# Every engine's attention and layer-norm steps in written order, and a rotation that multiplies in place

## The chip, the cores and the metric

The kernel runs on one core of one Trainium2 chip. The metric is the device time of one launch in microseconds (us). The kernel before was run three times: 1959.72, 1959.80 and 1962.09 us, median 1959.8.

## The reference

One step of a hybrid encoder layer for T = 320 token rows (256 of a prompt, 64 of a running sample), D = 2048, all in float32:

```python
xn = rmsnorm(x); h = xn @ w_in                      # columns [u | v | q | k | v_attn]
u, v = gelu(h[u]), gelu(h[v])                        # 2048 columns each
q, k = rope(h[q]), rope(h[k])                        # 32 query heads, 4 key heads, 64 wide; 16 rotated
a = u * (masked_ws @ layernorm(v) + bs)              # the gMLP branch, chunks of 128 rows
o = sink_softmax(q k^T / 8) v_attn                   # window of 128 keys and the own chunk of 64
x = x + (sigmoid(xn@w_gate_a) * (a @ w_branch_a) + sigmoid(xn@w_gate_b) * (o @ w_branch_b)) @ w_out
x = x + (silu(n@w_ffn_gate) * (n@w_ffn_up)) @ w_ffn_down,  n = rmsnorm(x);  y = rmsnorm(x)
```

The new keys, the new values and the normalised v rows of the sample are outputs too.

## The kernel before

Activations lie transposed, features on the partitions and the 320 rows along the free axis. Each weight product is three matmuls: a float32 operand is split into a rounded high part and the low rest (`xh`, `xl` for the activations, `hi`, `lo` for the weights), and hi·xh, hi·xl and lo·xh are added up in PSUM (L167 to L169).

**Blocks.** `gemm` (L151) makes 512 output columns with four PSUM banks. It goes through the 2048 inputs in eight blocks of 256, and a block is 24 matmuls. The weights of all products stand in one list `plan`, and block j uses entry j. At the start of block j ScalarE rounds the high part of entry j+2 (`high`, L134); after the first 12 matmuls VectorE subtracts to get the low part (`low`, L143) and SyncE fetches entry j+6 (`fetch`, L123). So a weight is to be ready two blocks ahead of its use.

**Slots.** After every 12 matmuls `pump` (L96) runs the functions that `later(n, fn)` has put n slots ahead. This calendar spreads the attention over the running products, two slots to a block. The products come in this order: kv, q0, q1, v0, q2, v1, q3, v2, v3 (list `QV`, L37), then the four of gate b (gb0 to gb3). Blocks are numbered from 0 through all of them, eight to a product, so v0 is blocks 24 to 31, q2 32 to 39, v1 40 to 47, q3 48 to 55, v2 56 to 63, v3 64 to 71, gb0 72 to 79.

**Attention.** A step (g, n) is key head g and chunk n of 64 rows, 20 steps in all, 5 slots apart within a g. `attend` (L475) places its parts at slots 0 to 16: scores on TensorE into two banks (slot 0), row maxima on VectorE (1, L492, then `nm` L494 and `es` L496), exponentials on ScalarE (2, L505, L508; these free the two banks), division on VectorE (3, L514 to L519) and ScalarE (4, L521), a transpose into `u` on VectorE (5, L527), four writes of `u` to DRAM by SyncE's queue (6, L536) and the read back as `pf` (8, L545), its high part on ScalarE (11, L557, L565) and low part on VectorE (12, L560, L568), the value matmuls on TensorE into one bank (14, L575), a copy `ol` on ScalarE (15, L579) and two additions into `f1` on VectorE (16, L587; these free the bank). When a q product ends, ScalarE copies it to `qr` (L600) and issues four small transfers that swap the two rotated halves into `swp` (L346, L347); at slots 5 and 7 VectorE turns two column tiles each (`rope_turn`, L349), and ScalarE and VectorE make the split queries `qs` (L467, L471). When a v product ends, VectorE scales it out of its four banks (L622), ScalarE applies Gelu (L625), and TensorE turns the four tiles (L630) into banks that VectorE and ScalarE copy out one slot later (L635, L636).

**Banks and rings.** There are eight PSUM banks: four for the running product and four for all else, the banks of the product before among them until they are copied out. The SBUF ring `st` has two buffers; `pf`, `ol` and `rope_t1` take them in turn.

**Layer norm.** During gb1 to gb3 `split_o` (L666) splits the attention's output, `v_aggr` (L670) and `v_norm` (L684) normalise v, `v_load` (L677) fetches gains and offsets, and `load_ws` (L691) and `turn_ws` (L699) fetch and turn the spatial weights.

**Order.** Inside `tc.manual_schedule()` every engine issues its instructions in the order in which the program writes them. In the kernel before this holds to the end of the kv product (L446). After it a scheduler orders each engine's instructions by its own forecast of when they can run: it takes the earliest written one that is ready by that forecast, so it moves instructions ahead of others that would wait. The order so fixed is what the chip runs.

Of the kernel before, what the change touches and what calls it, by code (L numbers as in the profile page):

```python
# [10 lines left out]
F32 = mybir.dt.float32  # L11
F32R = mybir.dt.float32r
AF = mybir.ActivationFunctionType
ALU = mybir.AluOpType
# [4 lines left out]
P = 128  # L19
D = 2048  # L20
DC = D // P
T = 320
# [47 lines left out]
def tile_hybrid_step(ctx: ExitStack, tc: tile.TileContext, a: dict, outs: list):  # L70
    nc = tc.nc
# [7 lines left out]
    tmp = ctx.enter_context(tc.tile_pool(name="tmp", bufs=2))  # L79
# [10 lines left out]
    def later(slots, fn):  # L90
        calendar.setdefault(now[0] + max(1, slots), []).append(fn)

    startup = tc.manual_schedule()
    startup.__enter__()

    def pump():  # L96
        now[0] += 1
        for fn in calendar.pop(now[0], []):
            fn()

    def flush():
        while calendar:
            pump()
# [47 lines left out]
    def gemm(w, c0, xh, xl, name, k0=0, nk=DC, nt=4):  # L151
        ps = [bank(f"mm_{name}_{t}") for t in range(nt)]
        for kb in range(0, nk, 2):
            j = at_block[0]
            at_block[0] += 1
            assert plan[j][1:] == (c0, k0 + kb, nt)
            ahead = j + PARTS - 1
            todo = ahead not in parts
            if todo:
                high(ahead)  # L160
            hi, lo = parts.pop(j)
            for t in range(nt):
                cols = slice(t * P, (t + 1) * P)
                for c in range(2):
                    k = kb + c
                    o = ps[t][:, :T]
                    nc.tensor.matmul(o, hi[:, c, cols], xh[:, k, :], start=(k == 0), stop=False)  # L167
                    nc.tensor.matmul(o, hi[:, c, cols], xl[:, k, :], start=False, stop=False)  # L168
                    nc.tensor.matmul(o, lo[:, c, cols], xh[:, k, :], start=False, stop=(k == nk - 1))  # L169
                if t == 1:  # L170
                    if todo:
                        low(ahead)
                    fetch(ahead + RAWS)
                if t % 2 == 1:
                    pump()
        return [p[:, :T] for p in ps]
# [163 lines left out]
    swp = ap.tile([P, 4, T], F32, name="swp")  # L340
    nc.gpsimd.memset(swp, 0.0)
    qr = ap.tile([P, 4, T], F32, name="qr")
# [4 lines left out]
            nc.scalar.dma_start(swp[b + 8 : b + 16, 0:nt, :], qr[b : b + 8, 0:nt, :])  # L347

    def rope_turn(t0):  # L349
        t1 = tmp.tile([P, 2, T], F32, tag="st", name="rope_t1")  # L350
        cb = cos_t.unsqueeze(1).broadcast_to([P, 2, T])
        sb = sin_t.unsqueeze(1).broadcast_to([P, 2, T])
        q2 = qr[:, t0 : t0 + 2, :]
        nc.vector.tensor_tensor(q2, q2, cb, op=ALU.mult)
        nc.vector.tensor_tensor(t1, swp[:, t0 : t0 + 2, :], sb, op=ALU.mult)
        nc.vector.tensor_tensor(q2, q2, t1, op=ALU.add)

    ka = ap.tile([P, 4, NPOS], F32R, name="ka")
    kl = ap.tile([P, 4, NPOS], F32R, name="kl")
# [83 lines left out]
            split_v64(5, v, 0)  # L443

    ps = gemm(w_in, 3 * D, xh, xl, "kv")
    startup.__exit__(None, None, None)  # L446
    for t in range(4):
        nc.scalar.activation(qr[:, t, :], ps[t], AF.Copy)
    later(1, lambda: rope_swap(2))
# [1 line left out]
    for i, n in xs:  # L451
        later(6 + i, lambda i=i, n=n: new_v(i, i * P, n))
        later(8 + 2 * i, lambda i=i: v_blocks(i))
    later(6, lambda: rope_turn(0))
    later(9, k_out)
    later(9, rope_scale)
# [141 lines left out]
    def q_done(g, ps):  # L598
        for t in range(4):
            nc.scalar.activation(qr[:, t, :], ps[t], AF.Copy)  # L600
        qs = ap.tile([P, 20, 2, 64], F32R, tag="qs", name=f"qs_{g}")
        hi, lo = q_parts(g, qs)
        later(1, lambda: rope_swap(4))
        later(5, lambda: rope_turn(0))
        later(7, lambda: rope_turn(2))
        at = QK0[g]
        later(at - 5, lambda: hi(0))
        later(at - 4, lambda: lo(0))
        later(at - 3, lambda: hi(1))
        later(at - 2, lambda: lo(1))  # L610
        for n in range(5):
            for dt, step in attend(g, n, qs, {}):
                later(at + 5 * n + dt, step)
# [107 lines left out]
    def sigmoid(dst, ps, b0, g):  # L721
        for t in range(4):
            m = 4 * g + t
            z = dst(m)
            nc.vector.tensor_tensor(z, ps[t], rx, op=ALU.mult)
            nc.scalar.activation(z, z, AF.Sigmoid, bias=vec[:, b0 + m : b0 + m + 1])
# [8 lines left out]
    for g in range(1, 4):  # L735
        sigmoid(gate_b, gemm(w_gate, D + g * W, xh, xl, f"gb{g}"), 80, g)
    flush()
    yh, yl = late["yh"], late["yl"]
    for g in range(4):
        ps = gemm(w_bb, g * W, yh, yl, f"bb{g}")  # L740
# [234 lines left out]
```

## Time and profile before

| | |
|---|---|
| median of three runs | 1959.8 us |
| the profiled execution | 1959.65 us, of which its span is 1957.5 us |
| TensorE busy | 1930.3 us (99%) |
| VectorE busy | 1041.6 us (53%) |
| ScalarE busy | 813.5 us (42%) |
| mean granted TensorE clock | 0.995 |
| read from HBM | 292.15 MB |

Times in the rows are microseconds from the start of the span, "mean ns" is one instruction's duration, "x" a count. PE is TensorE, PEld its weight loads, DVE VectorE, ACT ScalarE, SP SyncE; SPq and ACTq are those engines' queues of instructions and transfers. A row of the waits reads: who waited, for whom, us in total, times, the longest. L numbers are lines of the kernel.

### The profile page before, as it was taken

How to read it: one execution, taken by the hardware profiler on the slowest of the kernel's cores; microseconds unless marked ns; L12 is line 12 of the kernel's file. 1: busy time of each engine (PE TensorE's matmuls, PEld its weight loads, DVE VectorE, ACT ScalarE, POOL GpSimd, SP SyncE). 2: the span in 40 equal slices, each digit the busy share in tenths (PEclk: the TensorE clock that was granted, in tenths of full speed). 3: DMA queues.
4: the chain of work that ended last, by engine and by line, in shares of the span. 5: the costliest groups of instructions: out<-in, count | busy, mean ns of one | idle time of the engine just before them, and what ended most of it. 6: DMA issues, size and time to landing. Idle time of an engine off the chain costs nothing.

```text
span 1957.5 us, 31779 instructions
## 1 busy us (share of the span) xinstructions
PE 1930.3 (99%) x13179; PEld 1922.1 (98%) x13179; DVE 1041.6 (53%) x1527; ACT 813.5 (42%) x1220; POOL 4.7 (0%) x12
## 2 busy tenths in 40 slices
PE   8999999999999999999999999999999999999996
PEld 8999999999999999999999999999999999999996
DVE  5778887944354544455454434443444444444454
ACT  5566776533233343334343333333333333333343
POOL 0000000000000000000000000000000000000000
PEclk9999999999999999999999999999999999999998
DMA  8556666754444444445455555444555444555433
GB/s 261 162 161 184 175 179 177 225 159 146 149 143 136 140 151 151 151 150 203 147 149 151 151 151 151 151 150 147 148 150 150 150 151 151 151 151 149 149 129 103
DMA packets 169456, 307.41 MB, mean 157 GB/s; under 512 B 11312, under 2 KB 28672, under 8 KB 169120
## 3 DMA queue, kind: packets, MB, share of 16 engines
q1 hardware_dynamic: 164256, 293.64, 49.1%
q10 hardware_dynamic: 5056, 11.74, 1.9%
q8 instruction: 103, 1.69, 0.4%
q14 instruction: 41, 0.34, 0.0%
HBM read 292.15 MB, written 12.45 MB: 156 GB/s over the span
## 4 chain that ended last, share of the span: by engine, by line
PE 83%; DVE 1%; ACT 1%; DMA 1%; issue 0%; DVEq 0%; SPq 0%; ACTq 0%
PE mm_fd L169 5%; PE mm_fd L167 5%; PE mm_fu L167 5%; PE mm_fg L167 5%; PE mm_fg L168 5%; PE mm_fu L169 5%; PE mm_fg L169 5%; PE mm_fu L168 5%; PE mm_fd L168 5%; PE mm_u L167 2%; PE mm_ba L169 2%; PE mm_bb L167 2%; PE mm_ba L168 2%; PE mm_bb L168 2%; PE mm_ga L169 2%; PE mm_wo L169 2%
## 5 line engine op out<-in xcount | busy, mean ns | idle before, releaser
L143 DVE TENSOR_TENSOR lo<-raw,hi 128x1024 fp32r<-128x1024 f32 (+1 forms) x534 | 646.4, 1211 | 667.5 <-ACT hi L134 666.1
L134 ACT ACTIVATE hi<-raw 128x1024 fp32r<-128x1024 f32 (+1 forms) x533 | 559.3, 1050 | 1022.0 <-PE mm_fu L168 188.8
L167 PE MATMUL mm_fd<-xh,hi 128*128 128x320 f32 x704 | 218.2, 310 | 0.0
L167 PE MATMUL mm_fg<-yh,hi 128*128 128x320 f32 x704 | 217.8, 309 | 0.0
L168 PE MATMUL mm_fu<-yl,hi 128*128 128x320 f32 x704 | 217.6, 309 | 0.0
L169 PE MATMUL mm_fg<-yh,lo 128*128 128x320 f32 x704 | 217.6, 309 | 0.0
L168 PE MATMUL mm_fg<-yl,hi 128*128 128x320 f32 x704 | 217.6, 309 | 0.0
L167 PE MATMUL mm_fu<-yh,hi 128*128 128x320 f32 x704 | 217.6, 309 | 0.0
L169 PE MATMUL mm_fu<-yh,lo 128*128 128x320 f32 x704 | 217.6, 309 | 0.0
L169 PE MATMUL mm_fd<-xh,lo 128*128 128x320 f32 x704 | 217.1, 308 | 0.0
L168 PE MATMUL mm_fd<-xl,hi 128*128 128x320 f32 x704 | 217.1, 308 | 0.0
L168 PEld LDWEIGHTS mm_fg<-yl,hi 128*128 128x128 f32 x704 | 132.2, 188 | 0.1
L167 PEld LDWEIGHTS mm_fg<-yh,hi 128*128 128x128 f32 x704 | 132.2, 188 | 0.1
L167 PEld LDWEIGHTS mm_fu<-yh,hi 128*128 128x128 f32 x704 | 132.2, 188 | 0.0
L169 PEld LDWEIGHTS mm_fu<-yh,lo 128*128 128x128 f32 x704 | 132.2, 188 | 0.0
L169 PEld LDWEIGHTS mm_fg<-yh,lo 128*128 128x128 f32 x704 | 132.2, 188 | 0.0
L168 PEld LDWEIGHTS mm_fu<-yl,hi 128*128 128x128 f32 x704 | 132.2, 188 | 0.0
L168 PEld LDWEIGHTS mm_fd<-xl,hi 128*128 128x128 f32 x704 | 132.1, 188 | 0.0
L167 PEld LDWEIGHTS mm_fd<-xh,hi 128*128 128x128 f32 x704 | 132.1, 188 | 0.0
L169 PEld LDWEIGHTS mm_fd<-xh,lo 128*128 128x128 f32 x704 | 132.1, 188 | 0.0
L167 PE MATMUL mm_q<-xh,hi 128*128 128x320 f32 x256 | 80.7, 315 | 0.0
L167 PE MATMUL mm_u<-xh,hi 128*128 128x320 f32 x256 | 80.4, 314 | 0.0
(259 smaller groups left out, 3928.2 us busy)
## 6 DMA issues: line engine op xcount, KB each, us to landing
raw<-in_w_in_dram SPq DMA_DIRECT2D x104, 512.0 KB
raw<-in_w_ffn_gate_dram SPq DMA_DIRECT2D x88, 512.0 KB
raw<-in_w_ffn_up_dram SPq DMA_DIRECT2D x88, 512.0 KB
raw<-in_w_ffn_down_dram SPq DMA_DIRECT2D x82, 512.0 KB
raw<-in_w_gate_dram SPq DMA_DIRECT2D x64, 512.0 KB
raw<-in_w_branch_b_dram SPq DMA_DIRECT2D x32, 512.0 KB
raw<-in_w_branch_a_dram SPq DMA_DIRECT2D x32, 512.0 KB
raw<-in_w_out_dram SPq DMA_DIRECT2D x32, 512.0 KB
```

The costliest lines, as they stand in the source:

```text
L134: nc.scalar.activation(hi[:, :, :n], raws[j][:, :, :n], AF.Copy)
L143: nc.vector.tensor_tensor(lo[:, :, :n], raws.pop(j)[:, :, :n], f32(parts[j][0][:, :, :n]), op=ALU.subtract)
L167: nc.tensor.matmul(o, hi[:, c, cols], xh[:, k, :], start=(k == 0), stop=False)
L168: nc.tensor.matmul(o, hi[:, c, cols], xl[:, k, :], start=False, stop=False)
L169: nc.tensor.matmul(o, lo[:, c, cols], xh[:, k, :], start=False, stop=(k == nk - 1))
```

## The change

The region of written order ends after the last product of gate b and the flush behind it, instead of behind kv. It so takes in the four q and four v products, the whole attention, the layer norm and gate b. The rotation writes the product of the swapped half and the sine over `swp` itself, and `rope_t1` is gone from the ring `st`.

```diff
-    startup = tc.manual_schedule()
-    startup.__enter__()
+    ordered = tc.manual_schedule()
+    ordered.__enter__()
...
     def rope_turn(t0):
-        t1 = tmp.tile([P, 2, T], F32, tag="st", name="rope_t1")
         cb = cos_t.unsqueeze(1).broadcast_to([P, 2, T])
         sb = sin_t.unsqueeze(1).broadcast_to([P, 2, T])
-        q2 = qr[:, t0 : t0 + 2, :]
+        q2, s2 = qr[:, t0 : t0 + 2, :], swp[:, t0 : t0 + 2, :]
         nc.vector.tensor_tensor(q2, q2, cb, op=ALU.mult)
-        nc.vector.tensor_tensor(t1, swp[:, t0 : t0 + 2, :], sb, op=ALU.mult)
-        nc.vector.tensor_tensor(q2, q2, t1, op=ALU.add)
+        nc.vector.tensor_tensor(s2, s2, sb, op=ALU.mult)
+        nc.vector.tensor_tensor(q2, q2, s2, op=ALU.add)
...
     ps = gemm(w_in, 3 * D, xh, xl, "kv")
-    startup.__exit__(None, None, None)
...
     flush()
+    ordered.__exit__(None, None, None)
     yh, yl = late["yh"], late["yl"]
```

## The prediction

> **What bounds the kernel now.** I read the page, then the stretches, then TensorE's own waits.
>
> ```profile
> span 1957.5 us, 31779 instructions
> PE 1930.3 (99%) x13179; PEld 1922.1 (98%) x13179; DVE 1041.6 (53%) x1527; ACT 813.5 (42%) x1220; POOL 4.7 (0%) x12
> ```
>
> TensorE is busy all but 27 us, so the change can only gain what TensorE loses inside the region that it reorders, 47 to 435 us. The stretches put a size on that (columns: PE, PEld, DVE, ACT, POOL busy, clock, DMA share, GB/s):
>
> ```profile
> 100.00:150.00 50.00, 49.52 (x347) 49.10 (x346) 37.41 (x71) 32.13 (x75) 0.00 (x0) 1.00 0.58 167
> 150.00:200.00 50.00, 47.77 (x329) 47.20 (x330) 43.30 (x83) 33.35 (x88) 0.00 (x0) 1.00 0.63 182
> 200.00:250.00 50.00, 47.94 (x334) 47.21 (x333) 40.65 (x80) 35.09 (x83) 0.00 (x0) 1.00 0.63 176
> 250.00:300.00 50.00, 48.22 (x331) 46.87 (x330) 43.52 (x87) 35.49 (x87) 0.00 (x0) 1.00 0.64 185
> 300.00:350.00 50.00, 49.13 (x335) 48.24 (x335) 39.79 (x77) 35.13 (x70) 0.00 (x0) 1.00 0.59 175
> 350.00:435.00 85.00, 85.00 (x584) 84.98 (x582) 61.27 (x92) 37.88 (x50) 0.00 (x0) 1.00 0.62 192
> ```
>
> TensorE idles 0.48 + 2.23 + 2.06 + 1.78 + 0.87 = 7.4 us in the attention and nothing in the layer norm. **7.4 us is the most that the change can gain.** Who causes it:
>
> ```profile
> PE vt L630 <- ACT pr L505: 3.9, 3, 2.7
> PE o L575 <- ACT pr L505: 2.1, 1, 2.1
> PE o L575 <- DVE p L568: 1.0, 1, 1.0
> PE s L483 <- DVE qs L471: 0.5, 1, 0.5
> ```
>
> Transposes and value matmuls wait for the exponentials: these free the score banks, and no other bank is free. Behind the exponentials stands VectorE's `nm`. So VectorE is the second bound, 87% busy from 150 to 200 us (43.30 of 50), and TensorE stalls where VectorE is late by more than the calendar's lead.
>
> **The rotation.** It loses no instruction: eight products with the sine stay.
>
> ```profile
> L355 DVE TENSOR_TENSOR rope_t<-swp,sin_t 128x640 f32<-128x640 f32 x8 | 6.5, 818 | 0.0
> L354 DVE TENSOR_TENSOR qr<-qr,cos_t 128x640 f32<-128x640 f32 x8 | 6.5, 811 | 0.6 <-DMA swp<-qr 0.6
> ```
>
> L354 already multiplies in place and takes 811 ns, L355 into another tile 818 ns: 0 us, between -0.06 us (eight times 7 ns) and +0.06. What it frees is a place in the ring `st`: within one g, `pf` lives from slot 8 to 12 and the `ol` of the chunk before from slot 10 to 11 of the same count, which is two buffers. A third tenant would make a read back wait in written order; without it the ring costs nothing.
>
> **The layer norm.** The one transfer with a deadline is that of the spatial weights. It is issued far ahead of its written place:
>
> ```profile
> 360.84 0.39 ACTq L696 DMA_DIRECT2D wsr<-in_gmlp_ws_dram  x1
> 422.39 0.60 PE L702 MATMUL pw<-ident,wsr 128*128 128x128 f32 x4
> ```
>
> In written order it goes out in block 99, two blocks before block 101 turns it, some 7.8 us ahead (two blocks of 24 matmuls at 0.147 us, the two rows' spacing being 584 matmuls in 85 us, plus half a block, less one `hi`). It and `bsb` are 1.05 MB. Weights move at 512 KB in 3.52 us, 149 GB/s, and 333 GB/s is reached at the start (row below), so 184 GB/s remain: 5.7 us. Cost 0; at 130 GB/s, or if ScalarE were 2 us late, TensorE would wait up to 2 us. The rest has little work: VectorE 61 of 85 us.
>
> **The attention in written order.** TensorE's own stream changes next to nothing: in the trace its scores, transposes and values stand between the matmuls where the calendar writes them. VectorE and ScalarE change. The scheduler has moved work that was ready ahead of a `lo` or a maximum that was not. I work one stretch through, the turn from v1 to q3. First the prices:
>
> ```profile
> L143 DVE TENSOR_TENSOR lo<-raw,hi 128x1024 fp32r<-128x1024 f32 x100 | 121.6, 1218 | 53.9 <-ACT hi L134 53.3
> L134 ACT ACTIVATE hi<-raw 128x1024 fp32r<-128x1024 f32 x99 | 104.4, 1056 | 91.5 <-PE mm_gb L168 41.1 <-PE mm_v L168 13.7 <-PE mm_bb L168 12.2
> L505 ACT ACTIVATE pr<-s,nm 128x192 f32<-128x192 f32 x48 | 19.5, 417 | 11.6 <-DVE nm L494 8.4 <-PE mm_q L168 3.0
> L587 DVE TENSOR_TENSOR f<-o,ol 64x256 f32<-64x256 f32 x40 | 16.4, 410 | 1.4 <-ACT ol L579 1.1
> L492 DVE TENSOR_REDUCE mx<-s 128x2 f32<-128x384 f32 x24 | 12.7, 552 | 0.2
> L527 DVE STREAM_TRANSPOSE u<-pr 128x768 f32<-128x768 f32 x12 | 11.7, 971 | 1.0 <-ACT pr L521 1.0
> L519 DVE TENSOR_SCALAR pr<-pr,den 128x192 f32<-128x192 f32 x24 | 6.6, 316 | 0.2
> L560 DVE TENSOR_TENSOR pl<-pf,ph 128x512 fp32r<-128x512 f32 x16 | 11.0, 685 | 4.3 <-ACT ph L557 4.2
> ```
>
> ```profile
> 180.48 1.02 DVE L492 TENSOR_REDUCE mx<-s 128x2 f32<-128x384 f32 x2
> 181.54 0.17 DVE L494 SCALAR_TENSOR_TENSOR nm<-mx,nsink 128x4 f32<-128x4 f32 x1
> ...
> 189.12 1.22 DVE L143 TENSOR_TENSOR lo<-raw,hi 128x1024 fp32r<-128x1024 f32 x1
> 190.25 0.97 DVE L527 STREAM_TRANSPOSE u<-pr 128x768 f32<-128x768 f32 x1
> ```
>
> ```profile
> 180.84 0.63 ACTq L347 DMA_DIRECT2D swp<-qr  x1
> 181.57 1.06 ACT L134 ACTIVATE hi<-raw 128x1024 fp32r<-128x1024 f32 x1 [2.19 <-DMA swp<-qr]
> ```
>
> ```profile
> 196.41 0.69 DVE L560 TENSOR_TENSOR pl<-pf,ph 128x512 fp32r<-128x512 f32 x1
> ```
>
> ```profile
> 197.54 0.39 PE L575 MATMUL o<-ph,vv 128*128 128x512 f32 x1
> ```
>
> In a run of work the next instruction starts 0.08 us before the last one ends (189.12 + 1.22 against 190.25), so a `lo` counts 1.13, a `u` 0.9. ScalarE's four swap issues end at 181.5 in both orders, and the `hi` of entry 43 stands behind them, to 182.5. In before VectorE takes the maxima of (1,2) while that `hi` is awaited, from 180.48, and has `nm` at 181.7. In written order the `lo` of entry 43 stands ahead of these maxima: it waits for the `hi` and ends at 183.6, the maxima and `nm` at 184.8, `p2` of (1,0) at 185.6. ScalarE's four exponentials, 0.4 us each with their readings, and `es` end at 186.6; only then comes its next `hi`, to 187.5, and VectorE's `lo`, to 188.7, after an idle time of 1.9 us. Then, in written order: division (two small ones and two of L519) 0.85 (189.5), first rotation 2.2 (191.7), `lo` 1.13, `u` 0.9 (193.8), second rotation 2.2 (196.0), two additions 0.85, two maxima and two small ones 1.35 (198.2), `lo` 1.13 (199.3), `pl` 0.7: **200.0**. In before `pl` was moved ahead and began at 196.41; TensorE wants it at 197.54, so it waits **2.5 us** where it waited for nothing. This cannot be made up, since VectorE has no room there:
>
> ```profile
> 187.85:212.00 24.15, 24.15 (x168) 23.95 (x167) 23.68 (x45) 19.10 (x40) 0.00 (x0) 1.00 0.64 184
> ```
>
> It works 23.68 of 24.15 us, and the two gaps of 2 us that written order puts in front have to come out as waits. Going on in the same way, the four banks of v1 are copied out later, since the first of these copies stands behind the second `qs` instead of ahead of it: 0.7 us at q3's fourth bank. The wait of 2.1 us of `o` for the exponentials comes back at 2.4. This turn costs 2.5 + 0.7 + 2.4 - 2.1 = **+3.5 us**.
>
> The three other turns, worked with the same prices. v0 to q2: the exponentials come 1.0 us earlier, as v0's copies no longer cut in ahead of the division (the wait of 2.7 becomes 1.7), but `p2` of (0,3) ends 2.4 us after TensorE wants it: **+1.4**. v2: the second rotation stands ahead of `pl`, `p2` and the queries of g = 3, for waits of 1.0 and 1.75 us against 1.0 + 0.5: **+1.25**. v3 to gb0: a wait of 0.9 behind the exponentials goes, and `p2` of (3,3) is 2.0 us late: **+1.1**. The four make 3.5 + 1.4 + 1.25 + 1.1 = 7.25 us. But each walk starts from the state of before, and a microsecond that TensorE waits at one turn is one by which VectorE starts the next one less late; I take a fifth off for that, by choice: **+5.8 us**. Each figure may be off by two `lo`, 2.4 us, either way, since one handing-over decides it.
>
> **A rule weighed.** TensorE stands for 2.7 us behind 149 us, its longest wait, and the clock stays:
>
> ```profile
> 9.80:14.80 5.00, 5.00 (x21) 4.96 (x21) 1.70 (x3) 1.06 (x1) 0.00 (x0) 0.50 1.05 333
> 149.00:152.50 3.50, 0.79 (x6) 0.53 (x5) 3.36 (x6) 3.28 (x9) 0.00 (x0) 1.00 0.64 178
> 152.50:157.50 5.00, 5.00 (x36) 4.81 (x35) 4.90 (x10) 4.92 (x14) 0.00 (x0) 1.00 0.38 88
> ```
>
> Straight after the wait 36 matmuls fit into 5 us at a granted clock of 1.00; at the start, at 0.50, only 21. So a wait up to 2.7 us costs itself alone, and my 2.5 us are priced so. [...]
>
> **The rivals.** *A, the waits go.* The scheduler's forecast differs from the chip, and its moves cause the wait at 149 us: four copies of v0 run ahead of a division. If VectorE in written order reaches `pl` before TensorE does, all 7.4 us go: 1959.65 - 7.4 = 1952.2 us. For it: 53.3 us of `lo` waiting for `hi`, in the row of L143, which says that the moves leave gaps too. Against it: the walk, and VectorE's 98% from 188 to 212 us. It decides by the start of `pl` of (1,1): before 197.5 us A holds, at 200 the forecast. *B, an even trade.* The engines' orders differ by few places, and each late step gives VectorE the time to catch up, so the waits move and their sum stays: 1959.7 us. For it: three of the forecast's four terms are under 1.5 us, and each may be off by 2.4. Against it: the turn to q3, where a wait comes and none goes. [...] That the change does nothing is B.
>
> **The numbers.** Forecast, slower by 5.8 us: 1959.65 + 5.8 = 1965.5 us, chance 0.50. The profiled execution lies 0.15 us under the median of 1959.8, so no correction. A 0.18, B 0.22, C 0.10. About 0.2% (3.9 us) is what a measurement of this kernel can tell from no change. Of the forecast's 0.50, 0.05 falls under 3.9 us: same 0.22 + 0.05 = 0.27, slower 0.45 + 0.10 = 0.55, faster 0.18. The forecast's own range is 1960.7 to 1970.3 us (two of the four figures off together, 4.8 us). The range for 8 in 10 reaches three quarters into A (7.4 x 0.75 = 5.6: 1954) and, with one figure off by 2.4 us, past C (1974).
>
> **What would show it.** Right: in the changed profile TensorE idles some 13 us between 100 and 350 us; a row "PE o L575 <- DVE pl L560" or "<- DVE p L568" of 5 us or more; VectorE's `lo` waiting over 60 us for `hi`; the wait at 149 us shorter; 350 to 435 us still full; L355 at 0.81 us. [...]

## The result, and the profile after

The changed kernel takes 1980.1 us (median of 4 runs, 1979.55 to 1981.93), the kernel before beside it 1960.9 us (4 runs, 1959.72 to 1962.09): the ratio is 1.010, with a 95% interval of 1.0088 to 1.0112. It is slower by 19 us, where 5.8 us were forecast and 1974 us was the upper end. The profiled executions, 1959.65 us and 1980.11 us, differ by 20.5 us, their spans by 20.8 us.

The first part of the page after:

```profile
span 1978.3 us, 31760 instructions
PE 1940.2 (98%) x13179; PEld 1928.5 (97%) x13179; DVE 1046.3 (53%) x1527; ACT 814.4 (41%) x1220; POOL 4.7 (0%) x12
```

The work is the same, 13179 matmuls. TensorE's busy time has risen by 9.9 us, though, and not its idle time alone. The stretches show why (columns as before; the clock is the column ahead of the DMA share), first one stretch of before that had not been shown, then those of after:

```profile
50.00:100.00 50.00, 50.00 (x345) 49.47 (x344) 37.55 (x67) 29.86 (x56) 0.00 (x0) 1.00 0.53 156
```

```profile
50.00:100.00 50.00, 48.02 (x317) 47.16 (x317) 36.21 (x65) 28.74 (x55) 0.00 (x0) 0.97 0.49 139
150.00:200.00 50.00, 46.17 (x313) 44.40 (x312) 39.31 (x75) 31.39 (x77) 0.00 (x0) 1.00 0.55 158
200.00:250.00 50.00, 44.70 (x295) 43.34 (x294) 40.90 (x80) 33.13 (x78) 0.00 (x0) 0.97 0.57 161
250.00:300.00 50.00, 45.93 (x297) 44.15 (x297) 38.97 (x73) 31.03 (x73) 0.00 (x0) 0.97 0.60 174
300.00:350.00 50.00, 48.29 (x329) 46.40 (x328) 36.75 (x76) 34.76 (x83) 0.00 (x0) 1.00 0.58 169
350.00:400.00 50.00, 48.04 (x312) 47.59 (x313) 38.66 (x69) 29.66 (x47) 0.00 (x0) 0.97 0.57 170
400.00:435.00 35.00, 35.00 (x241) 35.00 (x240) 27.21 (x36) 12.66 (x15) 0.00 (x0) 1.00 0.61 185
```

From 50 to 400 us TensorE idles 1.98 + 3.83 + 5.30 + 4.07 + 1.71 + 1.96 = 18.9 us (100 to 150 us is full), where it was 7.4. That is 11.4 us more. Besides, four of these stretches have a granted clock of 0.97, where before had 1.00 throughout. Who causes the waits (TensorE's, 40 to 480 us):

```profile
PE o L573 <- DVE pl L558: 7.3, 5, 2.9
PE s L481 <- DVE qs L469: 2.5, 1, 2.5
PE vt L628 <- ACT pr L503: 2.2, 2, 1.2
PE o L573 <- ACT pr L503: 2.1, 1, 2.1
PE mm_q L167 <- ACT hi L134: 1.3, 1, 1.3
PE vt L628 <- DVE f L585: 0.9, 1, 0.9
PE o L573 <- DVE p L566: 0.8, 3, 0.3
PE mm_q L169 <- DVE lo L143: 0.7, 1, 0.7
...
```

The row of 7.3 us for `pl` is the one that the forecast named. Two rows are foreseen by nothing in it: `mm_q` waits for `hi` and `lo`, 2.0 us, at the end of q0. The 0.9 us for `f`, a bank that comes free late at 151 us, stand where the forecast had a wait for the exponentials.

**The turn that was walked through.** VectorE, then ScalarE, then TensorE, around the value matmul (1,1):

```profile
193.12 1.22 DVE L143 TENSOR_TENSOR lo<-raw,hi 128x1024 fp32r<-128x1024 f32 x1 [2.00 <-ACT hi L134]
...
205.14 0.68 DVE L558 TENSOR_TENSOR pl<-pf,ph 128x512 fp32r<-128x512 f32 x1
```

```profile
190.33 0.42 ACT L503 ACTIVATE pr<-s,nm 128x192 f32<-128x192 f32 x1 [1.99 <-DVE nm L492]
...
192.03 1.07 ACT L134 ACTIVATE hi<-raw 128x1024 fp32r<-128x1024 f32 x1
```

```profile
202.57 0.39 PE L573 MATMUL o<-ph,vv 128*128 128x512 f32 x1
205.88 0.50 PE L573 MATMUL o<-pl,vv 128*128 128x512 f32 x1 [2.92 <-DVE pl L558]
```

These rows show the two engines waiting for each other in turn: ScalarE stands 1.99 us for VectorE's `nm`, does four exponentials and only then its `hi`; VectorE stands 2.00 us for that `hi` (1.9 was forecast), with rotations, additions and `pl` written behind it. TensorE then waits 2.92 us for `pl` (2.5 forecast).

**What a wait does to the clock.** The switches of the granted clock lie on a grid: half clock from 76.54 to 79.95, 206.24 to 209.66, 284.75 to 288.16 and 353.02 to 356.43 us, each 3.41 us long, and the steps between are whole numbers of that: (206.24 - 79.95) / 3.41 = 37.0, (284.75 - 209.66) / 3.41 = 22.0, (353.02 - 288.16) / 3.41 = 19.0. With the four half clocks these are 82 periods, (356.43 - 76.54) / 82 = 3.4133 us each. Cut along that grid, the stretches of after read:

```profile
73.12:76.54 3.42, 1.44 (x8) 0.92 (x8) 2.55 (x7) 3.31 (x8) 0.00 (x0) 1.00 0.00 0
76.54:79.95 3.41, 3.41 (x14) 3.41 (x15) 2.98 (x8) 3.25 (x9) 0.00 (x0) 0.50 0.50 154
...
202.83:206.24 3.41, 0.49 (x3) 0.33 (x3) 3.27 (x9) 2.27 (x10) 0.00 (x0) 1.00 0.12 33
206.24:209.66 3.42, 3.42 (x15) 3.42 (x14) 2.63 (x4) 2.09 (x5) 0.00 (x0) 0.50 0.92 276
```

A period of 3.41 us with 1.98 us idle (3.42 - 1.44) or 2.92 us idle is followed by one at 0.50; the two others have 2.55 and 1.98 us idle ahead of them. The wait of 2.1 us behind 228 us lay across an edge, 1.35 us idle in the period from 226.72 us and 0.76 in the next, and cost no clock. So did the 2.7 us of before, on which the forecast had rested its price:

```profile
147.98:151.40 3.42, 1.54 (x11) 1.27 (x9) 3.33 (x5) 3.17 (x4) 0.00 (x0) 1.00 0.55 140
151.40:154.81 3.41, 2.58 (x17) 2.53 (x18) 3.25 (x10) 3.41 (x14) 0.00 (x0) 1.00 0.55 153
```

1.88 us idle on one side of the edge and 0.83 on the other. What a period at half clock costs is read from the step between two matmuls, inside one such period of after and behind it:

```profile
207.50 0.47 PE L169 MATMUL mm_v<-xh,lo 128*128 128x320 f32 x1
207.77 0.47 PE L167 MATMUL mm_v<-xh,hi 128*128 128x320 f32 x1
...
210.69 0.31 PE L169 MATMUL mm_v<-xh,lo 128*128 128x320 f32 x1
210.84 0.31 PE L167 MATMUL mm_v<-xh,hi 128*128 128x320 f32 x1
```

The step is 0.27 us (0.267 in the mean from 206.43 to 209.37 us) against 0.147. A period of 3.41 us so loses 3.41 x (1 - 0.147 / 0.267) = 1.5 us, an estimate from these two steps, and the four lose 6.1 us.

**The sum.** The column of matmuls counts what was lost: from 50 to 400 us there are 2353 in before and 2204 in after, and 149 x 0.147 = 21.9 us; ahead of that, in the first 47 us, after has 262 to 254, and 8 x 0.147 = 1.2 us come off again: 20.7 us, for the 20.8 between the spans. Of the 21.9 us, 11.4 us of idle time and 6.1 us of half clock make 17.5. Of the 4.4 that are left, a part lies at the edges of the stalls: `o<-pl` starts 3.31 us behind `o<-ph` (205.88 - 202.57), of which 2.92 are recorded as idle and 0.23 is the step from one value matmul to the next (the eight repeats in one experiment below take 1.98 us, less 0.39 for the last, over seven steps); 0.16 us is lost and shows nowhere. The trace records 19 waits in after and 6 in before; if each costs as much, 13 x 0.16 = 2.1 us. That is an estimate from one stall, and some 2.3 us stay open.

### The profile page after: what moved, and what is told of

Its sections match the earlier page's. It is cut to its first block, busy times and chain, and to the rows that moved or that the text cites. A ratio compares the mean times of both kernels' runs of the same rounds, so it can differ in the third digit from the quotient of the medians.

```text
span 1978.3 us, 31760 instructions
## 1 busy us (share of the span) xinstructions
PE 1940.2 (98%) x13179; PEld 1928.5 (97%) x13179; DVE 1046.3 (53%) x1527; ACT 814.4 (41%) x1220; POOL 4.7 (0%) x12
## 4 chain that ended last, share of the span: by engine, by line
PE 87%; DVE 5%; ACT 4%; DMA 2%; issue 1%; ACTq 0%; SPq 0%; DVEq 0%
PE mm_fd L169 5%; PE mm_fu L169 5%; PE mm_fg L169 5%; PE mm_fd L168 5%; PE mm_fg L168 5%; PE mm_fu L168 5%; PE mm_fu L167 5%; PE mm_fg L167 5%; PE mm_fd L167 5%; PE mm_u L167 2%; PE mm_bb L169 2%; PE mm_bb L168 2%; PE mm_ba L167 2%; PE mm_ga L167 2%; PE mm_wo L167 2%; PE mm_wo L168 2%
## 5 line engine op out<-in xcount | busy, mean ns | idle before, releaser
L167 PE MATMUL mm_v<-xh,hi 128*128 128x320 f32 x256 | 81.1, 317 | 0.2 <-ACT pr L503 0.2
```

## The experiments

The theory: in written order VectorE and ScalarE each stand at a step that waits for the other, with ready work written behind it; what TensorE needs comes 1 to 3 us late, and each period of 3.41 us with more than some 1.9 us idle (1.88 us kept the clock in before, 1.98 us lost it in after) costs a period of half clock. The ratios are against the kernel before, run beside each kernel on the same chip; its median there lay between 1960.1 and 1961.5 us, and the first row has the one beside after. "Idle" and "low" are TensorE's idle time and the periods of half clock between 50 and 400 us of the profile, "wait of lo" is VectorE's at `lo` for `hi` from 60 to 455 us.

| kernel | us | ratio (95% interval) | idle us | low | wait of lo us |
|---|---|---|---|---|---|
| before | 1960.9 | | 7.4 | 0 | 53.3 |
| after | 1980.1 | 1.010 (1.0088 to 1.0112) | 18.9 | 4 | 75.4 |
| rotation alone | 1959.1 | 0.9989 (0.9980 to 0.9998) | 6.4 | 0 | 48.3 |
| after, VectorE free | 1960.7 | 0.9997 (0.9988 to 1.0007) | 6.2 | 1 | 45.4 |
| VectorE ordered alone | 1966.0 | 1.0026 (1.0015 to 1.0037) | 7.7 | 2 | 57.8 |
| VectorE, ScalarE ordered | 1977.8 | 1.0088 (1.0072 to 1.0103) | 15.2 | 1 | 75.7 |
| `lo` behind the slot | 1962.5 | 1.0008 (0.9998 to 1.0017) | 7.2 | 2 | 48.4 |
| `lo` at the block's end | 1960.1 | 0.9996 (0.9987 to 1.0006) | 7.0 | 2 | 26.7 |
| values a slot later | 1982.1 | 1.0113 (1.0098 to 1.0128) | 20.6 | 4 | 79.1 |
| repeated matmuls in the waits | 1978.0 | 1.0084 (1.0069 to 1.0099) | 16.6 | 1 | 75.4 |
| cached keys later | 1978.3 | 1.0089 (1.0074 to 1.0104) | 16.7 | 4 | 74.7 |
| both repairs | 1958.1 | 0.9990 (0.9982 to 0.9999) | 5.3 | 1 | 29.2 |
| q0 free, `lo` at the end | 1954.2 | 0.9967 (0.9954 to 0.9979) | 3.2 | 0 | 31.4 |

**The rotation alone.** Edit to before: `rope_turn` as in the changed kernel; the order stays the scheduler's.

> The kernel before with the in-place rotation alone; the order stays the scheduler's after the keys and values. My theory (the written order of VectorE is what costs, the rotation costs nothing): 1959.8 us, within 2 us, and eight products with the sine of about 0.81 us each. Rival (the rotation costs: the swap of the next group must now wait until the rotation of this one has read its swapped half, or the freed ring place reorders the read-backs): 1965 us or more, with a wait in front of the swaps.

Measured 1959.1 us: the rival falls. The product in place takes 818 ns in the mean of nine (eight for the queries, one for the keys), as into a tile of its own in before.

The interval ends just under 1: in place is the faster by 0.4 to 3.9 us, and this run does not tell whether the free place in the ring does it. The loss of after is then the order's. Written order with the old rotation was not tried; by the forecast's walk its third tenant in the ring `st` would make a read back wait.

**Which engine's order.** Three edits: the startup region ends behind the keys and values as in before, and from there to the `flush` a region orders some engines only (names shortened here).

```diff
+    ordered.__exit__(None, None, None)
+    ordered = tc.manual_schedule(engines={PE, Activation, Pool, SP})   # then {DVE}, then {DVE, Activation}
+    ordered.__enter__()
```

> The changed kernel with written order on TensorE, ScalarE, SyncE and GpSimd, and VectorE alone left to the scheduler after the keys and values. My theory (VectorE standing at lo ahead of work that is ready is the cause): most of the loss goes, 1958 to 1966 us, TensorE idles 5 to 10 us between 50 and 400 us, and lo's waits for hi fall towards those of before. Rival (ScalarE's order is the cause: hi is written behind the exponentials and the copies, which wait for VectorE): 1975 us or more, with the same waits for pl.

> Written order on VectorE alone after the keys and values; TensorE, ScalarE, SyncE and GpSimd are left to the scheduler. With VectorE alone left to the scheduler the time was that of before, so VectorE's order is needed for the loss. My theory (it is also enough): 1974 to 1982 us, with the waits for pl. Rival (it takes ScalarE's written order as well, which puts a hi behind exponentials that wait for VectorE): 1960 to 1970 us.

> Written order on VectorE and ScalarE after the keys and values; TensorE, SyncE and GpSimd are left to the scheduler. VectorE alone cost 5 us, all engines but VectorE nothing, all together 20 us. My theory (the loss is in the pair: VectorE stands for a hi that ScalarE has behind exponentials, and these stand for VectorE): 1974 to 1982 us. Rival (TensorE's or SyncE's order is needed too): 1963 to 1970 us.

With VectorE alone left free the loss is gone (1960.7 us). So far the theory holds. But VectorE's order alone costs only 5.2 us, and there the rival was right: it takes ScalarE's too. The pair costs 17.7 us of the 19, so no other engine's order is needed. The stretches from 50 to 400 us, VectorE free, and then the pair:

```profile
50.00:400.00 350.00, 343.79 (x2349) 339.22 (x2349) 285.77 (x529) 226.52 (x489) 0.00 (x0) 1.00 0.60 176
```

```profile
50.00:400.00 350.00, 334.78 (x2233) 322.47 (x2232) 268.64 (x506) 220.30 (x486) 0.00 (x0) 1.00 0.58 166
```

2349 matmuls against 2233: 116 x 0.147 = 17.1 us. In the slow one VectorE works 268.64 of 350 us: with less of the work done in the same time it is also less busy, so over the whole stretch it was not full. Where one of the two has an order that the scheduler has fitted around the other's waits, all of the loss (VectorE free) or most of it (VectorE ordered alone) is hidden; two written orders that wait for each other hide nothing. The pair's waits are not those of after one by one, though: TensorE's for `pl` are 1.7 us instead of 7.3, and other waits, of up to 2.3 us for `hi`, have come. Its idle time is 7.8 us over that of before and it has one period of half clock, 1.5 us; by the count of matmuls it lost (2353 - 2233) x 0.147 = 17.6 us. Of the other 8 us, the edges of 16 more stalls would be 2.6 by the estimate above; the rest was not traced.

**The `lo` elsewhere.** If the standing at `lo` is the cause, it must be enough to write `lo` later, with every engine still in written order. In `gemm` (shown without the flag that limits it to the ordered region):

```diff
-                if t == 1:
-                    if todo:
-                        low(ahead)
-                    fetch(ahead + RAWS)
                 if t % 2 == 1:
                     pump()
+                if t == 1:      # second kernel: t == 3
+                    if todo:
+                        low(ahead)
+                    fetch(ahead + RAWS)
```

> The changed kernel, in which the lo of a block (and the fetch behind it) is written behind the slot's steps instead of ahead of them, in the ordered region only. My theory (VectorE stands at lo for a hi that ScalarE has behind its exponentials, with work that is ready written behind it): lo's waits for hi fall from 91 us between 40 and 480 us to under 60, pl of (1,1) is no later than TensorE's slot, TensorE idles under 12 us between 50 and 400 us, and the time is 1962 to 1970 us. Rival (VectorE is simply full in these stretches, so any order is late): TensorE's idle time stays at 16 us or more, 1975 us or more.

> As the last, but the lo stands at the end of the block, behind the steps of both of its slots, so that a hi has a whole block. My theory: lo's waits fall further, to under 40 us, and the time is 1958 to 1966 us; should the lo now come too late for its own matmuls, a row of matmuls waiting for lo of over 3 us appears. Rival (VectorE is full): 1975 us or more.

Both times came as the theory says, 1962.5 and 1960.1 us, and TensorE no longer waits for `pl` in either (the first rows of the second kernel, 40 to 480 us):

```profile
PE mm_q L170 <- DVE lo L144: 4.6, 2, 3.9
PE mm_v L170 <- DVE lo L144: 2.1, 2, 1.6
```

The wait of `lo` for `hi` between 40 and 480 us is 61.0 us and 38.6 us (91.1 in after; under 60 and under 40 were expected, so the first just misses). SyncE's `fetch` moves along with `lo` in these kernels; its order was not needed for the loss, as the pair above shows. The price is in the first row: at the end of q0, where keys and values fill ScalarE and VectorE, `lo` now comes too late for its own matmuls, 4.6 us, and two periods of half clock follow.

**A later value step.** In `attend`: (15, values), (16, lower), (17, total) for 14, 15, 16.

> The changed kernel with the value matmuls, the copy of their lower half and their sum one slot later (15, 16, 17 for 14, 15, 16), so that TensorE asks for pl 1.8 us later. My theory (each wait is one step that comes late by 1 to 3 us): the 8.1 us of waits for pl and p2 fall under 3 us, one or two periods of half clock go with them, and the time is 1968 to 1973 us. Rival (the lateness is VectorE's and turns up at the next thing that TensorE needs of it, a bank or a query): the waits for pl go, others of the same sum come, 1977 us or more.

The rival holds, 1982.1 us. The waits of after for `pl` shrink to 4.5 us, and others grow:

```profile
PE o L573 <- DVE pl L558: 4.5, 4, 2.7
PE s L481 <- DVE qs L469: 3.4, 1, 3.4
PE vt L628 <- DVE f L585: 2.6, 2, 1.7
...
PE s L481 <- ACT tok L634: 1.7, 1, 1.7
```

More lead for the step that waits does not help, since VectorE stays as late as it was; a bank comes free a slot later, and a query or a transpose waits instead.

**The clock by itself.** In `values` the first product of (1,1) is issued 8 times more, that of (3,3) 5 times more, as products of their own that the real one overwrites.

> The changed kernel, in which the first value matmul of (1,1) is issued 8 times more and that of (3,3) 5 times more. They only repeat the same product and fall into the time in which TensorE stands for pl (2.9 us and 1.7 us), so TensorE does more work and should arrive at the same moment. My theory (a stretch in which TensorE idles over some 1.9 us of 3.4 us is followed by 3.4 us at half clock, each costing 1.7 us): the stretches after these two waits run at a granted clock of 1.00 and the time falls by 2 x 1.7 us to 1976.7 us. Rival (the half clock is not set off by the idling, or it costs nothing since the next wait takes it back): 1980 us. If the repeats come out of TensorE's own time they would add 13 x 0.22 = 2.9 us: 1983 us.

The wait at (1,1) shrinks from 2.9 to 1.2 us, that at (3,3) from 1.7 to 0.5, and the periods behind them stay at 1.00 (the first, along the grid of this execution):

```profile
202.72:206.14 3.42, 2.60 (x13) 1.91 (x12) 3.31 (x8) 1.51 (x8) 0.00 (x0) 1.00 0.36 104
206.14:209.55 3.41, 3.02 (x22) 2.97 (x23) 3.33 (x7) 3.39 (x8) 0.00 (x0) 1.00 0.75 218
```

With 13 matmuls more the kernel is 2 us faster than after (1978.0 for 1980.1 us; the two intervals overlap by a little, so the gain rests on the rows as much as on the times). Half clock is left in one place only, between 250 and 300 us, where the mean clock is 0.97. The third missing one is luck, by estimate: the edge 37 periods ahead of the 202.72 us above lies at 76.43 us, and the first of the two waits at the end of q0 (1.3 and 0.7 us) ends at 75.12 us in after and some 1.3 us later here, so the edge falls between the two. Three periods at 1.5 us would be 4.6 us. In the profiled executions this kernel begins q0 1.3 us later than after (47.6 for 46.3 us) and comes to the turn of the spatial weights 2.3 us earlier (440.7 for 443.0), so between the two it gains 3.6; new waits of 0.5 us behind 88 us and of 0.3 us behind 219 us took most of the rest.

**The bound for the clock.** A kernel that computes none of the layer: trains of matmuls with rising standing times between.

> A kernel that leaves out the whole layer (it writes zeros): 62 trains of 62 to 84 matmuls of 128x320, and between two trains TensorE stands until VectorE has rewritten the weights, for times rising from about 1 us to about 3.3 us. My theory: the granted clock is taken over periods of 3.41 us on a fixed grid; a period with more than about 1.9 us idle is followed by one period at 0.50 and less leaves it at 1.00, so that the same standing time may or may not cost, by where it falls. Rival (one uninterrupted standing time over a whole period of 3.4 us is needed): no stretch after the start falls below 1.00, since every standing time here is shorter.

The theory holds: TensorE's longest wait for rewritten weights is 3.0 us, and yet the mean granted clock of the span of 857.2 us is 0.956. At 0.50 that is some 857.2 x (1 - 0.956) / 0.50 = 75 us, an estimate, where the 0.995 of before makes 20 in 1957.5 us. Two periods with nearly the same idle time, each with the one behind it:

```profile
167.20:170.61 3.41, 1.56 (x11) 1.30 (x9) 1.71 (x2) 0.00 (x0) 1.00 0.00 0
170.61:174.03 3.42, 3.38 (x23) 3.41 (x24) 0.00 (x0) 0.00 (x0) 1.00 0.00 0
576.80:580.21 3.41, 1.58 (x11) 1.35 (x10) 1.64 (x2) 0.00 (x0) 1.00 0.02 5
580.21:583.62 3.41, 3.41 (x15) 3.41 (x14) 0.00 (x0) 0.00 (x0) 0.50 0.00 0
```

Idle for 3.41 - 1.56 = 1.85 us kept the clock, 3.41 - 1.58 = 1.83 us lost it: these rows put the change at some 1.84 us of 3.41 in this kernel. In the layer it is less sharp. The period of before above kept the clock with 1.88 us idle, and one in the kernel with later values, below, lost it with 1.65 us (the next stands at 0.50):

```profile
310.05:313.46 3.41, 1.76 (x14) 1.59 (x13) 2.37 (x4) 2.34 (x6) 0.00 (x0) 1.00 0.11 34
```

**The end of q0, and the best version.** The cached keys' split moves from q0's slots to q1's:

```diff
-        later(4 + 3 * g, lambda g=g: put_cached_k(g))
+        later(18 + 3 * g, lambda g=g: put_cached_k(g))
```

> The changed kernel with the split of the cached keys alone moved, from q0 to q1 (the lo where the change has it). My theory: the two waits at the end of q0 (1.3 us for hi, 0.7 us for lo) and the half clock behind them go, and the turns stay: 1975 to 1978 us. Rival (the next turn takes it back, or q1 is now too full): 1979 us or more.

1978.3 us, at the edge between the two: the wait for `hi` is gone, that of 0.7 us for `lo` stays, and there is no half clock in q0. But the half clock behind 283 us lasted two periods in this profile, so there are four as in after.

> The changed kernel with the lo at the end of its block from q1 on (in q0 where it was) and the cached keys split in q1 instead of in q0. My theory (in written order two places cost: a lo written ahead of work that is ready, and ScalarE and VectorE overfull with keys and values at the end of q0): with both mended TensorE idles under 4 us between 50 and 400 us, no period of half clock is left there, and the time falls under that of before, 1952 to 1957 us. Rival (the repairs only move the waits, as a later value step did): 1960 us or more.

1958.1 us: the repairs do more than move the waits, but TensorE stands 3.2 us for `lo` in the q products, 2.5 of them at 85.9 us in q1, where the moved keys now meet the late `lo`; a period of half clock follows. So the theory was missed in all three: 1957 us by 1 us, 5.3 us idle for under 4, and one period for none.

> The changed kernel with q0 left to the scheduler and written order from q1 on, with the lo at the end of its block there. My theory: the loss at the end of q0 (2 us of waits and 1.7 us of half clock) is the scheduler's to avoid, as in before, and the attention keeps the 2 to 3 us of idle time that the late lo left: 1953 to 1958 us. Rival (the waits move): 1960 us or more.

Here the `__enter__` stands behind q0's matmuls, `lo` at t == 3 from there on. It takes 1954.2 us, 5.9 us under the 1960.1 us of before beside it, and beats both kernels. Its first waits and its stretch:

```profile
PE mm_v L170 <- DVE lo L144: 2.6, 2, 2.0
PE vt L634 <- ACT pr L509: 0.4, 1, 0.4
```

```profile
50.00:400.00 350.00, 346.77 (x2382) 342.56 (x2382) 286.60 (x525) 229.74 (x493) 0.00 (x0) 1.00 0.62 178
```

2382 matmuls in the stretch where before had 2353. Of the 7.4 us that the forecast called the most that could be gained, 4.2 are recovered. So written order as such was not the loss; the place of one step in it was.

## Why the forecast was too low

**What held.** The direction, the mechanism and the place: TensorE waits where the walk put it. For `pl` of (1,1) 2.9 us (2.5 forecast), for the exponentials at 228 us 2.1 (2.4), for the queries of g = 3 2.5 us and for (2,2) 1.3 (1.75 and 1.0), for (3,3) 2.0 (2.0), at 148 to 155 us 2.1 (1.7) and at (0,3) 1.6 (2.4). The 0.7 us at q3's fourth bank did not come; a wait of 1.0 us for the exponentials at 304 us, and some under 0.4, came that the walk does not have. VectorE's `lo` waits 75.4 us for `hi` (over 60). The rotation's product takes 817 ns; the layer norm costs nothing, 400 to 435 us being full and no wait of TensorE following up to 480, and the spatial weights are issued 8.75 us ahead of their turn at 443.0 us (7.8 forecast):

```profile
434.25 0.39 ACTq L694 DMA_DIRECT2D wsr<-in_gmlp_ws_dram  x1
```

**What failed.** First, "a wait up to 2.7 us costs itself alone". This was drawn from one wait that happened to lie across an edge of the grid. In four periods the idle time, in one wait or two, added up to 1.98 to 2.92 us, and each cost 1.5 us more, 6.1 us. C, which has 0.10 of the chances and the upper end of the range, stood for a clock that falls behind one longer wait; no run shows a length of one wait at which it falls. What the runs show in its place is the idle time within one period of 3.41 us: 1.98 us were enough in after and 1.83 us in the kernel of trains, while a wait of 2.7 us across an edge cost no clock in before. Second, "a fifth off" because waits would be made up at the next turn: the sum shows no such making up. The waits at the four turns stand 9.4 us above those of before (11.4 less the 2.0 of q0), where 7.25 were worked out. Third, the end of q0 was left out. The steps of the keys and values were walked past because TensorE was full there; in written order ScalarE's splits of keys stand ahead of its `hi`:

```profile
73.34 0.31 ACT L386 ACTIVATE ka<-ck 64x128 fp32r<-64x128 f32 x1
73.68 0.31 ACT L387 ACTIVATE ka<-ck 64x128 fp32r<-64x128 f32 x1
74.01 1.06 ACT L134 ACTIVATE hi<-raw 128x1024 fp32r<-128x1024 f32 x1
```

TensorE wanted that `hi` 1.3 us earlier. Fourth, a smaller one: "VectorE has no room there" holds of the stretch in before, 23.68 of 24.15 us, but is not what makes `pl` late: with `lo` moved, the order still written, TensorE does not wait for `pl`.

To the 5.8 us forecast, 1.45 come back for the fifth, 2.15 for larger waits, 2.0 for q0 and 6.1 for the clock: 17.5 us. The 4.4 us beyond, the edges of stalls by estimate and an open rest, less 1.2 us of a faster start, make the 20.7. Rival A fell at its own point: `pl` of (1,1) began 205.14 us, 2.3 us behind TensorE's slot, which was at 202.8. Rival B fell with the sum.

## What to carry to other kernels

When a scheduler's order is replaced by the written one, look for pairs of engines that wait for each other within one step, and write the consumer's half (here `lo`) well behind the producer's (`hi`), with ready work between; giving the late step more lead downstream only moved the wait. Price a wait of TensorE by where it falls as well as by its length: here the clock was lost with 1.65 us of idle time in one period of 3.41 us and kept with 1.88 in another, and each period of half clock cost some 1.5 us on top. Where one place is overfull, leave that place to the scheduler and order the rest.

## What the runs showed of the hardware

In the profile of after the granted clock changed on a grid of 3.4133 us, and between the kernels the edges are not tied to the program: the half clock of the start ends at 14.86 us in before and at 15.10 in after, and one begins at 286.16 us in the kernel with later values, which modulo 3.4133 us is 1.21, 1.45 and 2.86 us. So one and the same wait may cost its length in one execution and some 1.5 us more in another: the two waits at the end of q0, 1.28 and 0.71 us, lost the clock in after (0.50 from 76.54 us), and with repeated matmuls, where by the estimate above an edge fell between them, they did not (1.00 from 50 to 100 us). In five of the kernels above a half clock lasted two periods instead of one: VectorE ordered alone (201.88 to 208.71 us), `lo` behind the slot (215.73 to 222.56), `lo` at the block's end (76.85 to 83.67), values a slot later (286.16 to 292.99) and cached keys later (283.65 to 290.48). In the last two and in `lo` behind the slot that was so although the first period was busy throughout (3.41 of 3.41 us). Ahead of it stood as much idle time as elsewhere ahead of one: 2.55 us in the kernel with cached keys later, two periods, and 2.55 us at 281.34 us of after, one. What makes it stay was not found.
